# Conv products behind the query and key projections, four spread tiles in memory at once, scores ahead of the value projection

## The chip, the cores and the metric

One core of a Trainium2 chip runs the whole program. The time is device microseconds of one execution, and the median of three runs is compared. The core has five engines with an instruction queue each: TensorE (PE, matrix products), VectorE (DVE), ScalarE (ACT), GpSimd (POOL) and SyncE (SP, which here only issues loads). Each engine takes its instructions in order, and one that waits holds up all behind it. DMA transfers are issued from the queues of SP, ACT and POOL.

## The reference

One layer of an encoder with 256 tokens of width 1024, all in fp32. `mod` is six vectors of 1024 from the conditioning `c`.

```python
mod = silu(c) @ w_ada + b_ada                 # shift1, scale1, gate1, shift2, scale2, gate2
h = rms_norm(x, norm1_g) * (1 + scale1) + shift1
proj = h @ w_in                               # conv pair 2*512 | q 512 | k 512 | v 512
conv_out = conformer_conv(...)                # a*sigmoid(g), depthwise conv of width 31, layer norm, swish
attn_out = diff_attention(q, k, v, ...)       # 4 heads, normed q and k, two softmaxes each, p0 - lam * p1
x = x + gate1 * (concat([conv_out, attn_out]) @ w_out)
h2 = rms_norm(x, norm2_g) * (1 + scale2) + shift2
x = x + gate2 * routed_experts(h2, ...)       # top 4 of 32 experts, clamped SwiGLU, weights by softmax
```

## The kernel before

The order of instructions on each engine is the order in which the program is written (`manual_schedule` over all five engines). The front part, up to about 214.8 us, computes everything up to the routing; the rest runs the 32 experts one after the other.

**Weights.** All large weights come in chunks of 1 MB (`chunk`, L68; `wchunk`, L598), issued by SP in program order into rings of slots: `ringA` with 8 slots, `ringW` with 4, and from the close of `early` on `ringB` with 7. A load waits until the slot's former contents have been used, and the ones behind it wait too. An expert takes 12 chunks (8 of gate and up, 4 of down). The first experts' chunks go into slots that hold modulation weights (`ADA`), so `mod` frees them.

**Modulation.** `mod(s, q)` (L196) computes a quarter of vector s on DVE: two multiplies of 128x1024 with a running sum (L199) and a small add (L204). There are 24 of them, one for each ADA chunk, spread over the front part. The last six stand in the residual loop (`MODS`, L639).

**Conv.** The GLU writes `pad` (L320), one group of 128 channels j after another in the order `JS` = 2, 3, 1, 0. `spread(j)` (L264) copies a group into a tile `xs` by 16 small DMAs with four shifts, so that `conv(j)` (L272) can do the 31 taps as 32 short products on PE. Two `xs` buffers exist, so the third spread waits for the first conv. `spread(2)` is issued by ACT, the three others by POOL. `conv(j)` writes the one PSUM buffer `pc`, and ACT copies it to `acc`(L279); the next user of `pc` waits for that copy.

**Attention.** `proj(w, t)` (L334) projects q, k and v (w = 0, 1, 2) for two halves t of the tokens. `head_squares`, `head_norm` and `head_turn` normalise q and k and turn them; `scores`, `softmax`, `difference`, `turn_p` and `attend` do one head each. `out_proj(d, i, ...)` (L539) adds half i of the mix to output group d. In the last loop (L641) each d gets its second half, `residual(d)` on DVE adds it to x, `route(d)` on PE adds to the router's scores, and `add_squares` (L619) sums squares for the second norm.

**Biases of the experts.** `bgu` (32x2048, fp32) is split into three bfloat16 parts in `b3` (rows 0, 32 and 64): ACT copies the first part (L445), DVE subtracts it (L453), ACT copies the rest to `b3m` (the buffer named `osb`, L454), DVE subtracts again (L459), and ACT copies the remainder (L471).

Names in the trace: `pc` is the PSUM buffer of conv and of `turn_p`, `pq` that of the projections, of scores and of out_proj; `s` at L453 is `bgu`; `xT` also holds the residual.

Of the kernel before, what the change touches and what calls it, by code (L numbers as in the profile page):

```python
# [4 lines left out]
F32 = mybir.dt.float32  # L5
# [8 lines left out]
T = 256  # L14
# [17 lines left out]
def hybrid_layer(tc, xT_d, par_d, ada_d, win_d, wout_d, bgu_d, bdn_d, wgu_d, wdn_d, out_d):  # L32
# [44 lines left out]
    def load_ada(s, q):  # L77
        ADA[s, q] = chunk(ada_d[s, q])
# [14 lines left out]
    for q in range(4):  # L93
        load_ada(1, q)
        load_ada(0, q)
        WI[0, q] = chunk(win_d[q])
    for c in range(2):
        WI[1, c] = chunk(win_d[4 + c])
    load_ada(4, 0)
    load_ada(4, 1)  # L100
    nc.sync.dma_start(bgu, bgu_d)
    for c in range(2):
        WI[2, c] = chunk(win_d[6 + c])
    load_ada(4, 2)
    load_ada(4, 3)
    for c in range(2):
        WI[3, c] = chunk(win_d[8 + c])

    fold_w = [ringW.tile([128, 2048], F32, name="w") for i in range(2)]
    for q in range(4):  # L110
        load_ada(3, q)


    dgrid = mid.tile([128, 128], I32, name="dgrid")
# [107 lines left out]
    def scale1(q):  # L222
        ks = slice(2 * q, 2 * q + 2)
        V.scalar_tensor_tensor(a1[:, ks], modT[:, 1, ks], 1.0, pc("n1", 2 * q, 2 * q + 2), op0=OP.add, op1=OP.mult)

    r1 = rms_scale(ss1, 2, NT, "1")
    mod(1, 0)
    scale1(0)
    mod(0, 0)
    for i in range(12):  # L230
# [32 lines left out]

    def spread(j):  # L264

        XS[j] = early.tile([128, 4, T + 28], F32, name="xs", bufs=2)
        for i in range(4):
            for b in range(4):
                (nc.scalar if j == 2 else G).dma_start(XS[j][32 * i:32 * i + 32, b],
                                                       pad[32 * b:32 * b + 32, j, i:i + T + 28])  # L270

    def conv(j):  # L272
        pcn = ps_s.tile([128, T], F32, name="pc")
# [24 lines left out]
    for q in range(4):  # L298
        if q:
            mod(1, q)  # L300
            scale1(q)
            mod(0, q)
        norm_x(q)
        make_h(q)
        if q == 0:
            A.activation(dist, dist, AF.Abs)
        elif q == 1:
            for h in range(2):
                A.activation(alibi[:, h], dist, AF.Copy, scale=-SLOPES[h])
        elif q == 2:  # L310
            for h in range(2, 4):
                A.activation(alibi[:, h], dist, AF.Copy, scale=-SLOPES[h])
        else:
            table(AF.Sigmoid)
        for j in JS:
            conv_in(q, j)
            if q == 3:
                sg = early.tile([128, T], F32, name="qn", bufs=2)
                A.activation(sg, pcv[j][:, 1], AF.Sigmoid)
                V.tensor_mul(pad[:, j, 15:15 + T], pcv[j][:, 0], sg)  # L320
                if j in (2, 3):
                    spread(j)
                if j == 3:
                    make_folds(0)
    close(ps_c)
# [101 lines left out]
            TE.transpose(pt[:, t], osb[:, 2 * h + t], identf)  # L427
        A.activation(mixT[:, 4 + h], pt.rearrange("p a b -> p (a b)"), AF.Copy, scale=sg8)

    WO[0] = [chunk(wout_d[0, c], ringW) for c in range(2)]  # L430
    load_ada(2, 0)
    load_ada(2, 1)
    first, second = range(4), range(4, KD)
    proj(0, 0)
    mod(4, 0)
    head_squares(0, 0)
    conv(2)
    spread(1)
# [4 lines left out]
    V.tensor_scalar(sg8, pc("sg"), 1.0 - LAM0, None, op0=OP.mult)  # L443
    mod(4, 1)
    A.activation(b3[0:32], bgu, AF.Copy)  # L445
    proj(0, 1)
    conv(3)
    spread(0)
    mod(4, 2)
    head_squares(0, 1)  # L450
    head_norm(0)
    conv(1)
    V.tensor_sub(bgu, bgu, b3[0:32])  # L453
    A.activation(b3m, bgu, AF.Copy)  # L454
    mod(4, 3)
    proj(1, 0)
    for t in range(NT):
        head_turn(0, t)
    V.tensor_sub(bgu, bgu, b3m)  # L459
    A.activation(b3[32:64], b3m, AF.Copy)  # L460
    head_squares(1, 0)
    conv(0)
    mu = ps_s.tile([128, T], F32, name="po")
    for j in JS:
        TE.matmul(mu, mean512, acc[:, j], start=j == JS[0], stop=j == JS[-1])
    mod(3, 0)
    proj(1, 1, first)
# [3 lines left out]
    A.activation(b3[64:96], bgu, AF.Copy)  # L471
# [5 lines left out]
    mod(3, 1)  # L477
    proj(1, 1, second)
    WO[1] = [chunk(wout_d[1, c], ringW) for c in range(2)]
    load_ada(2, 2)  # L480
    load_ada(2, 3)
    for q in range(4):
        load_ada(5, q)
# [4 lines left out]
    head_squares(1, 1)  # L488
    head_norm(1)
    proj(2, 0, first)  # L490
    rbc = ps_s.tile([128, T], F32, name="po")
    for t in range(NT):
        TE.transpose(rbc[:, t * 128:t * 128 + 128], rv[:, t:t + 1].to_broadcast([128, 128]), identf)
    for j in range(4):
        V.tensor_mul(acc[:, j], acc[:, j], rbc)
        A.activation(sqc[:, j, :T], acc[:, j], AF.Sigmoid, scale=pc("lg", j), bias=pc("lb", j))
        V.tensor_scalar(acc[:, j], acc[:, j], pc("lg", j), pc("lb", j), op0=OP.mult, op1=OP.add)
    proj(2, 0, second)
    for t in range(NT):
        head_turn(1, t)  # L500
    for i in range(2):
        V.tensor_mul(lp[:, i], pc("lam", 128 * i, 128 * i + 64), pc("lam", 128 * i + 64, 128 * i + 128))
    V.tensor_reduce(lam, lp, axis=AX.X, op=OP.add)
    A.activation(lam, lam, AF.Exp)
    A.activation(vt[:, 0], PQ[2, 0], AF.Copy)
    for j in range(4):
        V.tensor_mul(mixT[:, j], acc[:, j], sqc[:, j, :T])
    PQ[2, 1] = ps_s.tile([128, 512], F32, name="pq", bufs=4)
    scores(0, "pq")
    scores(1, "pt")  # L510
    proj(2, 1)
    nlam = mid.tile([128, 1], F32, name="nlam")
    V.tensor_sub(nlam, lam[:, 1:2], lam[:, 0:1])
    V.tensor_scalar(nlam, nlam, -LAM0, None, op0=OP.add)
    softmax(0)
    softmax(1)
    mod(3, 2, (0,))
    difference(0)
    A.activation(vt[:, 1], PQ[2, 1], AF.Copy)
# [555 lines left out]
```

## Time and profile before

| | us |
|---|---|
| median of three runs | 1196.76 (1194.98, 1196.76, 1197.84) |
| profiled execution, its time | 1198.14 |
| its span | 1196.4 |
| PE busy | 1091.1 (91%) |
| DVE busy | 338.3 (28%) |
| ACT busy | 146.5 (12%) |
| POOL busy | 25.7 (2%) |
| first gate product of expert 0 | 214.81 |
| mean granted TensorE clock | 0.977 of full speed |

The busy shares are means over two very different parts. In the experts PE is nearly always busy; in the front part it is idle for some stretches and its granted clock falls to half in some of them, seen in products that take twice as long (L277: 64 products in 3.66 us or in 7.06). In a timeline row the first number is the start, the second the time from there to the end of the group, then engine, line, operation, output<-inputs, the size, the count, and in brackets the idle time before it with what ended it. A name with q behind the engine (SPq, ACTq) is its queue.

### The profile page before, as it was taken

How to read it: one execution, taken by the hardware profiler on the slowest of the kernel's cores; microseconds unless marked ns; L12 is line 12 of the kernel's file. 1: busy time of each engine (PE TensorE's matmuls, PEld its weight loads, DVE VectorE, ACT ScalarE, POOL GpSimd, SP SyncE). 2: the span in 40 equal slices, each digit the busy share in tenths (PEclk: the TensorE clock that was granted, in tenths of full speed). 3: DMA queues.
4: the chain of work that ended last, by engine and by line, in shares of the span. 5: the costliest groups of instructions: out<-in, count | busy, mean ns of one | idle time of the engine just before them, and what ended most of it. 6: DMA issues, size and time to landing. Idle time of an engine off the chain costs nothing. (4 is left out here: it accounts for less than half of the span.)

```text
span 1196.4 us, 13803 instructions
## 1 busy us (share of the span) xinstructions
PE 1091.1 (91%) x5387; PEld 498.3 (42%) x5387; DVE 338.3 (28%) x833; ACT 146.5 (12%) x301; POOL 25.7 (2%) x57
## 2 busy tenths in 40 slices
PE   7969878999999999998999999998988988898886
PEld 4625466534443344443444444443333333333332
DVE  7354667322222122221222222222111122222212
ACT  2013321110011000110000101000000000000000
POOL 0052000000000000000000000000000000000000
PEclk8978898999999999999999999999999999999999
DMA  9795528999999899997799999999999999999993
GB/s 376 274 344 200 207 102 318 421 419 420 419 419 422 337 412 419 421 420 298 296 414 420 418 419 420 420 419 421 419 420 420 419 421 419 419 420 419 419 401 133
DMA packets 65892, 449.36 MB, mean 376 GB/s; under 512 B 7984, under 2 KB 8496, under 8 KB 12240
## 3 DMA queue, kind: packets, MB, share of 16 engines
q1 hardware_dynamic: 63424, 445.27, 91.1%
q0 software_dynamic: 1584, 1.88, 0.5%
q8 instruction: 83, 1.36, 0.5%
q10 hardware_dynamic: 768, 0.58, 0.2%
q14 instruction: 33, 0.27, 0.1%
HBM read 444.33 MB, written 1.05 MB: 372 GB/s over the span
## 5 line engine op out<-in xcount | busy, mean ns | idle before, releaser
L772 PE MATMUL pu<-w,xg 128*64 128x512 f32 x1024 | 234.8, 597 | 19.8 <-DMA w<-in_wgu_dram 19.8
L772 PE MATMUL pg<-w,xg 128*64 128x512 f32 x1024 | 232.0, 597 | 13.0 <-DMA w<-in_wgu_dram 8.1
L813 PE MATMUL pd<-w,yT 128*64 128x512 f32 x992 | 218.1, 592 | 0.0
L772 PEld LDWEIGHTS pg<-w,xg 128*64 128x64 f32 x1024 | 79.2, 136 | 163.4 <-issue 139.8
L772 PEld LDWEIGHTS pu<-w,xg 128*64 128x64 f32 x1024 | 75.4, 136 | 153.2 <-issue 99.9
L813 PEld LDWEIGHTS pd<-w,yT 128*64 128x64 f32 x992 | 69.5, 137 | 127.9 <-issue 123.9
L965 DVE COPY o<-pd 64x512 f32<-64x512 f32 x31 | 21.2, 683 | 224.8 <-PE pd L813 224.8
L777 DVE TENSOR_SCALAR gp<-pg 128x512 f32<-128x512 f32 x34 | 23.5, 691 | 215.3 <-PE pg L772 215.3
L786 DVE TENSOR_SCALAR gp<-pu 128x512 f32<-128x512 f32 x32 | 22.1, 692 | 175.4 <-issue 163.6
L734 PEld LDWEIGHTS misc<-hot,xtok 128*128 128x128 f32 x496 | 57.8, 192 | 12.3 <-issue 12.2
L750 PE MATMUL y<-s,o 128*128 128x256 f32 x240 | 59.0, 389 | 4.2 <-PEq L947 0.6
L734 PE MATMUL misc<-hot,xtok 128*128 128x128 f32 x496 | 62.0, 278 | 0.0
L199 DVE SCALAR_TENSOR_TENSOR w<-w,crow 128x1024 f32<-128x1024 f32 x48 | 56.7, 1217 | 3.4 <-DMA w<-in_ada_dram 3.4
L750 PEld LDWEIGHTS y<-s,o 128*128 128x128 f32 x240 | 43.1, 189 | 16.3 <-issue 11.7
L967 ACT ACTIVATE o<-pd 64x512 f32<-64x512 f32 x31 | 18.4, 593 | 254.7 <-DVE o L965 254.7
L780 ACT ACTIVATE sg<-gp 128x512 f32<-128x512 f32 x32 | 20.1, 630 | 231.1 <-DVE gp L777 231.1
L338 PE MATMUL pq<-w,hT 128*128 128x512 f32 x96 | 42.9, 596 | 0.0
L277 PE MATMUL pc<-xs,w 128*32 128x256 f32 x256 | 23.7, 482 | 14.1 <-DVE pad L320 6.8
L542 PE MATMUL pq<-mixT,w 128*128 128x256 f32 x128 | 31.6, 398 | 5.1 <-DVE xT L613 5.1
L257 PE MATMUL cv<-hT,w 128*128 128x256 f32 x128 | 30.9, 408 | 5.6 <-DVE hT L246 5.6
L710 ACT ACTIVATE xg<-misc,modT,a 128x128 f32<-128x128 f32 x62 | 28.3, 457 | 45.9 <-DVE xg L712 45.9
L797 ACT ACTIVATE yT<-pu 128x256 f32<-128x256 f32 x32 | 12.3, 383 | 174.5 <-PEq L947 155.6
(291 smaller groups left out, 701.2 us busy)
## 6 DMA issues: line engine op xcount, KB each, us to landing
w<-in_wgu_dram SPq DMA_DIRECT2D x256, 1024.0 KB, 19.9
w<-in_wdn_dram SPq DMA_DIRECT2D x124, 1024.0 KB, 19.9
w<-in_ada_dram SPq DMA_DIRECT2D x24, 1024.0 KB, 10.8
w<-in_win_dram SPq DMA_DIRECT2D x10, 1024.0 KB, 12.3
w<-in_wout_dram SPq DMA_DIRECT2D x4, 1024.0 KB, 8.7
w<-in_wdn_dram SPq DMA_DIRECT2D x8, 512.0 KB, 14.5
xs<-pad POOLq DMA_DIRECT2D x48, 35.5 KB, 6.1
xT<-in_xT_dram SPq DMA_DIRECT2D x2, 512.0 KB, 5.8
```

The costliest lines, as they stand in the source:

```text
L199: V.scalar_tensor_tensor(w, w, 1.0, crow, op0=OP.mult, op1=OP.mult, accum_out=modT[:, s, 2 * q + i:2 * q + i + 1])
L257: TE.matmul(pcv[j][:, g], WI[0, q][:, o:o + 128], hT[:, k], start=k == 0 and g == 0, stop=k == KD - 1, skip_group_check=True)
L277: TE.matmul(pcn[32 * b:32 * b + 32], fold_w[j // 2][:, o:o + 32], XS[j][:, b, 4 * g:4 * g + T], start=g == 0, stop=g == 7)
L338: TE.matmul(PQ[w, t], hT[:, k, t * 128:t * 128 + 128], WI[1 + w, k // 4][:, (k % 4) * 512:(k % 4) * 512 + 512], start=k == 0, stop=k == KD ...
L542: TE.matmul(po4[d // 2][:, d % 2], WO[i][k // 2][:, o:o + 128], mixT[:, 4 * i + k], start=first and k == 0 and d % 2 == 0, stop=last and k ...
L710: A.activation(dst, src, AF.Identity, scale=a2[:, k:k + 1], bias=sh2[:, k:k + 1])
L734: TE.matmul(px[:, i], xtok[:, t, k * 128:k * 128 + 128], PP[p][:, t], start=t == 0, stop=t == NT - 1)
L750: TE.matmul(Y[d // 2][:, d % 2], O[p][:, d * 128:d * 128 + 128], S[p].rearrange("p a b -> p (a b)"), start=False, stop=False, skip_group_c ...
L772: TE.matmul(P[64 * n:64 * n + 64], xg[:, k], W[k // 2][:, o:o + 512], start=False, stop=k == KD - 1)
L777: V.tensor_scalar(gp, P, 7.0, None, op0=OP.min)
L786: V.tensor_scalar(y, P, -7.0, 7.0, op0=OP.max, op1=OP.min)
L813: TE.matmul(P[64 * n:64 * n + 64], yT[:, j, half * 64:half * 64 + 64], down_part(W, f, n), start=f == 0, stop=f == 7)
```

## The change

The code is written in another order and a few instructions change engine.

- `spread` writes groups 2 and 3 into `ringW` tiles and groups 1 and 0 into the two `xs` buffers, and is called for every group right behind its `pad`; all its DMAs are issued by POOL.
- All four `conv` calls stand behind the q and k projections: `conv(2)` and `conv(3)` behind `proj(1, 1)`, `conv(1)` behind the turn of k, `conv(0)` behind `scores(0)`. Scores 0 and 1 stand ahead of the value projections.
- The two subtractions of the bias split go from DVE to POOL; the affine step of the conv's norm goes from DVE to ACT.
- The modulations are placed earlier: the loop holds four of them (5, 0 to 3). The first is split, with one half ahead of the first norm chain. In the loop `add_squares` stands ahead of `residual`.
- The order of the loads follows; `WO[0]` is loaded into the slots that the two spread tiles held, `WO[1]` into those of the fold weights.
- `turn_p(2)` and `turn_p(3)` stand behind one out_proj pair each, `softmax(2)` behind the attends of the first two heads.

```diff
@@ loads @@
-    load_ada(4, 0)
-    load_ada(4, 1)
...
+    for w in (1, 2):
+        for c in range(2):
+            WI[w, c] = chunk(win_d[2 + 2 * w + c])
+        if w == 1:
+            nc.sync.dma_start(bgu, bgu_d)
+    for q in range(4):
+        load_ada(4, q)
+    load_ada(3, 0)
     for c in range(2):
         WI[3, c] = chunk(win_d[8 + c])
+    for q in range(1, 4):
+        load_ada(3, q)
+    load_ada(2, 0)
+    load_ada(2, 1)
@@ first norm @@
+    mod(1, 0, (0,))
     r1 = rms_scale(ss1, 2, NT, "1")
-    mod(1, 0)
+    mod(1, 0, (1,))
@@ def spread(j) @@
-        XS[j] = early.tile([128, 4, T + 28], F32, name="xs", bufs=2)
+        if j < 2:
+            XS[j] = early.tile([128, 4, T + 28], F32, name="xs", bufs=2)
+        else:
+            XS[j] = ringW.tile([128, 2048], F32, name="w")[:, :4 * (T + 28)].rearrange("p (b t) -> p b t", b=4)
...
-                (nc.scalar if j == 2 else G).dma_start(XS[j][32 * i:32 * i + 32, b],
-                                                       pad[32 * b:32 * b + 32, j, i:i + T + 28])
+                G.dma_start(XS[j][32 * i:32 * i + 32, b], pad[32 * b:32 * b + 32, j, i:i + T + 28])
...
-                if j in (2, 3):
-                    spread(j)
+                spread(j)
@@ projections @@
     A.activation(b3[0:32], bgu, AF.Copy)
+    G.tensor_tensor(bgu, bgu, b3[0:32], OP.subtract)
     proj(0, 1)
-    conv(3)
-    spread(0)
-    mod(4, 2)
     head_squares(0, 1)
     head_norm(0)
+    A.activation(b3m, bgu, AF.Copy)
+    G.tensor_tensor(bgu, bgu, b3m, OP.subtract)
+    proj(1, 0)
...
+    proj(1, 1)
+    A.activation(b3[32:64], b3m, AF.Copy)
+    A.activation(b3[64:96], bgu, AF.Copy)
+    head_squares(1, 1)
+    head_norm(1)
+    conv(2)
+    conv(3)
...
+    conv(1)
...
+    scores(0, "pq")
...
+    conv(0)
+    WO[0] = [chunk(wout_d[0, c], ringW) for c in range(2)]
+    load_ada(2, 2)
+    load_ada(2, 3)
+    WO[1] = [chunk(wout_d[1, c], ringW) for c in range(2)]
...
+    scores(1, "pt")
...
+    proj(2, 0, first)
...
+    proj(2, 1, first)
...
     for u in range(4):
         attend(u)
-    mod(3, 2, (1,))
+    softmax(2)
     softmax(3)
@@ residual loop @@
-    MODS = {0: (2, 2), 1: (2, 3), 3: (5, 0), 4: (5, 1), 6: (5, 2), 5: (5, 3)}
+    MODS = {0: (5, 0), 2: (5, 1), 4: (5, 2), 5: (5, 3)}
...
         out_proj(d, 1, range(4), last=True)
+        if before_d:
+            add_squares(before_d)
         residual(d)
```

POOL around the spreads, before (L269 is the spread, L610 a constant for the last norm):

```order
L118 IOTA sqq 128x512
L269 DMA xs<-pad 32x284 x48
L610 MEMSET ones_1128 128x1
L910 DMA o<-in_bdn_dram 32x1024
L927 UNCONDITIONAL_BRANCH
```

The same place after; s_85 is `bgu`, b_283 the tile `b3`, osb the tile `b3m`:

```order
L119 IOTA sqq 128x512
L274 DMA w<-pad 32x284 x32
L274 DMA xs<-pad 32x284 x32
L444 TENSOR_TENSOR s_85<-s_85,b_283 32x2048
L449 TENSOR_TENSOR s_85<-s_85,osb 32x2048
L616 MEMSET ones_1136 128x1
```

All 64 spread DMAs stand on POOL, and the two subtractions stand behind them.

ACT from the GLU's first sigmoid on, before (qn is the sigmoid, sqq a square of `head_squares`, acc the copy behind a conv, the rows into b_279 and osb the bias copies):

```order
L319 ACTIVATE qn<-cv_276 128x256
L269 DMA xs<-pad 32x284 x16
L319 ACTIVATE qn<-cv_277 128x256
L319 ACTIVATE qn<-cv_275 128x256
L319 ACTIVATE qn<-cv_274 128x256
L345 ACTIVATE sqq<-pq 128x512
L279 ACTIVATE acc<-pc,par 128x256
L445 ACTIVATE b_279<-s_85 32x2048
L279 ACTIVATE acc<-pc,par 128x256
L345 ACTIVATE sqq<-pq 128x512
L279 ACTIVATE acc<-pc,par 128x256
L454 ACTIVATE osb<-s_85 32x2048
```

ACT from the second square on, after:

```order
L348 ACTIVATE sqq<-pq 128x512
L448 ACTIVATE osb<-s_85 32x2048
L348 ACTIVATE sqq<-pq 128x512
L365 ACTIVATE qT<-pt,gq_290 128x4x128 x2
L461 ACTIVATE b_283<-osb 32x2048
L462 ACTIVATE b_283<-s_85 32x2048
L348 ACTIVATE sqq<-pq 128x512
L283 ACTIVATE acc<-pc,par 128x256 x2
L365 ACTIVATE kT<-pt,par 128x4x128 x2
```

The copies behind conv(2) and conv(3) (acc) stand behind the three bias copies that need the differences, where two of them stood ahead of the first such copy.

PE from the first projection on, before (pq is a projection, pc a conv, pt the turn of q, po a mean of the conv's norm):

```order
L338 MATMUL pq<-w,hT 128x512 x8
L277 MATMUL pc<-xs,w 32x256 x32
L338 MATMUL pq<-w,hT 128x512 x8
L277 MATMUL pc<-xs,w 32x256 x64
L338 MATMUL pq<-w,hT 128x512 x8
L360 MATMUL pt<-identf,qn 128x128 x8
L277 MATMUL pc<-xs,w 32x256 x32
L465 MATMUL po<-acc,mean_79 128x256 x4
```

The same place after (pc<-w is conv(2) and conv(3), whose spread tiles are slots named w; the second pt is the turn of k, the last pq are scores):

```order
L341 MATMUL pq<-w,hT 128x512 x24
L363 MATMUL pt<-identf,qn 128x128 x8
L341 MATMUL pq<-w,hT 128x512 x8
L281 MATMUL pc<-w 32x256 x64
L363 MATMUL pt<-identf,qn 128x128 x8
L281 MATMUL pc<-xs,w 32x256 x32
L375 MATMUL pq<-kT,qT 128x256 x4
```

All four projections of q and k stand ahead of the first conv.

DVE in the residual loop, before (L613 is the residual, L199 and L204 a modulation, L620 the sum of squares):

```order
L613 SCALAR_TENSOR_TENSOR xT<-pq,modT,xT 128x256
L199 SCALAR_TENSOR_TENSOR w,modT<-w,crow 128x1024 x2
L204 TENSOR_TENSOR modT<-modT,par 128x2
L613 SCALAR_TENSOR_TENSOR xT<-pq,modT,xT 128x256
L199 SCALAR_TENSOR_TENSOR w,modT<-w,crow 128x1024 x2
L204 TENSOR_TENSOR modT<-modT,par 128x2
L613 SCALAR_TENSOR_TENSOR xT<-pq,modT,xT 128x256
L620 TENSOR_TENSOR s2all<-s2all,s_1144 128x256
L613 SCALAR_TENSOR_TENSOR xT<-pq,modT,xT 128x256
```

The same place after:

```order
L619 SCALAR_TENSOR_TENSOR xT<-pq,modT,xT 128x256
L200 SCALAR_TENSOR_TENSOR w,modT<-w,crow 128x1024 x2
L205 TENSOR_TENSOR modT<-modT,par 128x2
L619 SCALAR_TENSOR_TENSOR xT<-pq,modT,xT 128x256
L626 TENSOR_TENSOR s2all<-s2all,s_1152 128x256
L619 SCALAR_TENSOR_TENSOR xT<-pq,modT,xT 128x256
L200 SCALAR_TENSOR_TENSOR w,modT<-w,crow 128x1024 x2
L205 TENSOR_TENSOR modT<-modT,par 128x2
```

Two of the six modulations left the loop, and the sum of squares stands ahead of the next residual.

## Rows read from the trace of the kernel before

**Rows 1.** waits of PE, 215 to 820 (line waited for: us, times, longest).
```profile
PE misc L762 <- ACT xg L710: 5.5, 2, 2.7
```

**Rows 2.** timeline of PE (start, us, instructions, idle before).
```profile
214.81 5.32 PE L772 MATMUL pg<-w,xg 128*64 128x512 f32 x24
...
348.34 7.09 PE L772 MATMUL pg<-w,xg 128*64 128x512 f32 x32 [0.17 <-PEq L968]
```

**Rows 3.** waits of the load queue SPq, 300 to 410.
```profile
SPq L600 <- PE pd L813: 17.0, 2, 16.7
```

**Rows 4.** busy time by stretch: PE, PEld, DVE, ACT, POOL, PEclk, DMA share, GB/s.
```profile
400.00:420.00 20.00, 18.90 (x92) 7.59 (x90) 3.21 (x9) 1.22 (x2) 0.00 (x0) 1.00 0.73 293
600.00:1160.00 560.00, 518.39 (x2494) 208.37 (x2490) 118.47 (x272) 51.75 (x105) 0.00 (x0) 1.00 1.01 419
```

**Rows 5.** timeline of SPq, issues of loads.
```profile
59.47 3.83 SPq L70 DMA_DIRECT2D w<-in_ada_dram  x2
...
73.82 21.36 SPq L70 DMA_DIRECT2D w<-in_ada_dram  x4
...
320.63 17.70 SPq L600 DMA_DIRECT2D w<-in_wgu_dram  x8
```

**Rows 6.** page, section 6: issues, KB each, us from issue to landing.
```profile
w<-in_wgu_dram SPq DMA_DIRECT2D x256, 1024.0 KB, 19.9
```

**Rows 7.** waits of PE, 45 to 214.
```profile
PE pc L277 <- DVE pad L320: 6.8, 1, 6.8
PE pc L277 <- DMA xs<-pad: 6.6, 2, 6.2
PE pq L542 <- DVE xT L613: 5.1, 2, 4.2
```

**Rows 8.** timeline of ACT, 45 to 100.
```profile
45.99 14.11 ACTq L269 DMA_DIRECT2D xs<-pad  x16
...
98.68 1.89 ACT L454 ACTIVATE osb<-s 32x2048 bf16<-32x2048 f32 x1
```

**Rows 9.** timeline of POOL, 0 to 100.
```profile
1.33 0.59 POOL L118 IOTA sqq<- 128x512 f32 x1
61.29 4.07 POOL L269 DMA_DIRECT2D xs<-pad  x8 [59.38 <-DVE pad L320]
...
72.19 1.08 POOL L269 DMA_DIRECT2D xs<-pad  x2 [0.39 <-DMA xs<-pad]
...
91.35 5.91 POOL L269 DMA_DIRECT2D xs<-pad  x12 [0.29 <-DMA xs<-pad]
```

**Rows 10.** timeline of DVE.
```profile
10.93 0.16 DVE L125 TENSOR_SCALAR rm<-ss 128x2 f32<-128x2 f32 x1 [1.83 <-PE ss L218]
...
90.26 2.27 DVE L453 TENSOR_TENSOR s<-s,b 32x2048 f32<-32x2048 f32 x1
```

**Rows 11.** page, section 5: groups (busy us, mean ns, idle before).
```profile
L199 DVE SCALAR_TENSOR_TENSOR w<-w,crow 128x1024 f32<-128x1024 f32 x48 | 56.7, 1217 | 3.4 <-DMA w<-in_ada_dram 3.4
...
L338 PE MATMUL pq<-w,hT 128*128 128x512 f32 x96 | 42.9, 596 | 0.0
```

**Rows 12.** timeline of PE, 80 to 185.
```profile
81.32 3.66 PE L277 MATMUL pc<-xs,w 128*32 128x256 f32 x64
91.21 7.06 PE L277 MATMUL pc<-xs,w 128*32 128x256 f32 x64 [6.22 <-DMA xs<-pad]
...
145.20 1.13 PE L372 MATMUL pq<-kT,qT 64*128 64x256 f32 x8
...
151.03 7.07 PE L542 MATMUL pq<-mixT,w 128*128 128x256 f32 x32
159.01 0.41 PE L405 MATMUL pc<-identf,s 128*128 128x128 f32 x2 [0.91 <-DVE s L397]
...
173.27 1.97 PE L542 MATMUL pq<-mixT,w 128*128 128x256 f32 x8
179.42 3.50 PE L542 MATMUL pq<-mixT,w 128*128 128x256 f32 x8 [4.18 <-DVE xT L613]
```

More of the change, by code (lines that the diff above doesn't have):

```diff
@@ L96, in hybrid_layer @@
         WI[0, q] = chunk(win_d[q])
-    for c in range(2):
-        WI[1, c] = chunk(win_d[4 + c])
-    load_ada(4, 0)
-    load_ada(4, 1)
[L101 to L105, printed above, removed]
+    for w in (1, 2):
[6 more added lines that the diff above has]
+    load_ada(3, 0)
     for c in range(2):
         WI[3, c] = chunk(win_d[8 + c])
+    for q in range(1, 4):
+        load_ada(3, q)
+    load_ada(2, 0)
+    load_ada(2, 1)
     fold_w = [ringW.tile([128, 2048], F32, name="w") for i in range(2)]
-    for q in range(4):
-        load_ada(3, q)
     dgrid = mid.tile([128, 128], I32, name="dgrid")
@@ L428, in head_mix @@
         A.activation(mixT[:, 4 + h], pt.rearrange("p a b -> p (a b)"), AF.Copy, scale=sg8)
-    WO[0] = [chunk(wout_d[0, c], ringW) for c in range(2)]
-    load_ada(2, 0)
-    load_ada(2, 1)
     first, second = range(4), range(4, KD)
@@ L436, in hybrid_layer @@
     head_squares(0, 0)
-    conv(2)
-    spread(1)
     V.tensor_scalar(identb, dgrid, 0.0, None, op0=OP.is_equal)
@@ L445, in hybrid_layer @@
     A.activation(b3[0:32], bgu, AF.Copy)
+    G.tensor_tensor(bgu, bgu, b3[0:32], OP.subtract)
     proj(0, 1)
-    conv(3)
-    spread(0)
-    mod(4, 2)
     head_squares(0, 1)
     head_norm(0)
-    conv(1)
-    V.tensor_sub(bgu, bgu, b3[0:32])
     A.activation(b3m, bgu, AF.Copy)
-    mod(4, 3)
+    G.tensor_tensor(bgu, bgu, b3m, OP.subtract)
     proj(1, 0)
+    mod(4, 2, (0,))
+    head_squares(1, 0)
     for t in range(NT):
         head_turn(0, t)
-    V.tensor_sub(bgu, bgu, b3m)
-    A.activation(b3[32:64], b3m, AF.Copy)
-    head_squares(1, 0)
-    conv(0)
+    mod(4, 2, (1,))
+    mod(4, 3)
+    for i in range(2):
+        V.tensor_mul(lp[:, i], pc("lam", 128 * i, 128 * i + 64), pc("lam", 128 * i + 64, 128 * i + 128))
+    V.tensor_reduce(lam, lp, axis=AX.X, op=OP.add)
+    proj(1, 1)
+    A.activation(b3[32:64], b3m, AF.Copy)
+    A.activation(b3[64:96], bgu, AF.Copy)
[3 more added lines that the diff above has]
+    conv(3)
+    mod(3, 0)
+    mod(3, 1)
+    mod(3, 2, (0,))
+    for t in range(NT):
+        head_turn(1, t)
+    conv(1)
+    PQ[2, 0] = ps_s.tile([128, 512], F32, name="pq", bufs=4)
+    PQ[2, 1] = ps_s.tile([128, 512], F32, name="pq", bufs=4)
+    scores(0, "pq")
+    A.activation(lam, lam, AF.Exp)
+    nlam = mid.tile([128, 1], F32, name="nlam")
+    V.tensor_sub(nlam, lam[:, 1:2], lam[:, 0:1])
+    V.tensor_scalar(nlam, nlam, -LAM0, None, op0=OP.add)
+    softmax(0)
+    mod(3, 2, (1,))
+    conv(0)
+    WO[0] = [chunk(wout_d[0, c], ringW) for c in range(2)]
+    load_ada(2, 2)
+    load_ada(2, 3)
+    WO[1] = [chunk(wout_d[1, c], ringW) for c in range(2)]
+    for q in range(4):
+        load_ada(5, q)
     mu = ps_s.tile([128, T], F32, name="po")
@@ L465, in hybrid_layer @@
         TE.matmul(mu, mean512, acc[:, j], start=j == JS[0], stop=j == JS[-1])
-    mod(3, 0)
-    proj(1, 1, first)
+    scores(1, "pt")
     V.tensor_sub(acc, acc, mu[:, None, :].to_broadcast([128, 4, T]))
@@ L470, in hybrid_layer @@
     A.activation(sqc[:, :, :T], acc, AF.Square)
-    A.activation(b3[64:96], bgu, AF.Copy)
+    proj(2, 0, first)
     vsr = ps_s.tile([128, T], F32, name="po")
@@ L476, in hybrid_layer @@
     A.activation(vrow, vsr, AF.Copy)
[L477 to L483, printed above, removed]
+    softmax(1)
+    difference(0)
+    mod(3, 3)
+    proj(2, 0, second)
+    A.activation(vt[:, 0], PQ[2, 0], AF.Copy)
     vs = ps_s.tile([128, 2], F32, name="po")
@@ L487, in hybrid_layer @@
     rv = rms_scale(vs, 1, NT, "c")
-    head_squares(1, 1)
-    head_norm(1)
-    proj(2, 0, first)
+    difference(1)
+    table(AF.Sigmoid)
+    proj(2, 1, first)
     rbc = ps_s.tile([128, T], F32, name="po")
@@ L496, in hybrid_layer @@
         A.activation(sqc[:, j, :T], acc[:, j], AF.Sigmoid, scale=pc("lg", j), bias=pc("lb", j))
[L497 to L505, printed above, removed]
+    turn_p(0)
+    for j in range(4):
+        A.activation(acc[:, j], acc[:, j], AF.Identity, scale=pc("lg", j), bias=pc("lb", j))
+    mod(2, 0)
+    proj(2, 1, second)
+    A.activation(vt[:, 1], PQ[2, 1], AF.Copy)
     for j in range(4):
         V.tensor_mul(mixT[:, j], acc[:, j], sqc[:, j, :T])
[L508 to L519, printed above, removed]
+    table(AF.Exp)
+    turn_p(1)
     scores(2, "pq")
-    turn_p(0)
-    difference(1)
     scores(3, "pt")
-    turn_p(1)
-    softmax(2)
     for u in range(4):
         attend(u)
-    mod(3, 2, (1,))
+    softmax(2)
     softmax(3)
@@ L549, in hybrid_layer @@
         out_proj(d, 0, range(4), True)
+    turn_p(2)
+    difference(3)
     next_po()
@@ L552, in hybrid_layer @@
         out_proj(d, 0, range(4), True)
-    difference(3)
-    turn_p(2)
+    mod(2, 1)
+    turn_p(3)
     next_po()
-    for d in (4, 5):
-        out_proj(d, 0, range(4), True)
-    turn_p(3)
+    out_proj(4, 0, range(4), True)
     for u in range(4, 8):
         attend(u)
+    out_proj(5, 0, range(4), True)
     head_out(1)
@@ L566, in hybrid_layer @@
         head_mix(h)
-    mod(3, 3)
+    mod(2, 2)
     V.scalar_tensor_tensor(a2, modT[:, 4], 1.0, pc("n2"), op0=OP.add, op1=OP.mult)
@@ L578, in hybrid_layer @@
                   start=k == 0, stop=k == KD - 1)
-    mod(2, 0)
-    mod(2, 1)
+    mod(2, 3)
     V.tensor_add(rbias, sb, pc("br"))
@@ L647, in hybrid_layer @@
             route(before_d)
-            if before_d:
-                add_squares(before_d)
         before_d = d
```

## Prediction

> **What bounds the kernel now.** I read the waits of TensorE (PE) first, in the expert part. From 215 to 820 us its longest wait is 5.5 us in two pieces, on ScalarE (ACT), and no weight load stands in that list [rows 1]: PE sets the pace there. Next, who waits for PE: in 300 to 410 the load queue (SP) stood 17.0 us on PE's down products [rows 3], and the DMA engines were 0.73 busy in 400 to 420 [rows 4], where an expert runs a second block of tokens: the weight rings were full and the loads could not run ahead. After 600 the DMA is at 1.01 [rows 4]; from there loads set the pace. So the loads of the last part start when PE frees slots at the extra blocks, and that is a fixed distance behind the first gate product of expert 0, at 214.81 [rows 2]. If that product comes X us earlier, the end comes X us earlier, as long as weights still arrive ahead of PE. The tightest place I found is expert 5: its load group was issued from 320.63 on [rows 5], a load lands 19.9 us after its issue [rows 6], so 340.5, and is used at 348.34 [rows 2]: 7.8 us to spare. If the loads move earlier as much as the products, the 7.8 stays; if they don't move, X counts only to 7.8.
>
> The change touches only the front part. There PE's largest waits are 6.8 us on the padded GLU outputs (the spreads' source), 6.6 on spread DMAs and 5.1 on the residual in the last loop [rows 7]. All three are touched.
>
> **Start.** VectorE (DVE) idles 1.83 us ahead of the first norm chain [rows 10]. Half of a modulation, 1.2 us [rows 11], now fills it. One of its two multiplies leaves the path, less the handover: 0.8 earlier (0 to 1.2).
>
> **Spreads.** ACT spent 14.11 us issuing 16 spread DMAs [rows 8] while the sigmoids of the next groups waited behind it, which is PE's 6.8. Now GpSimd (POOL) issues all 64, each group right behind its pad, and no tile is waited for. POOL's pace is seen twice: 16 from 61.29 to 73.27, 0.75 each, while weight loads are in flight, and 12 in 5.91, 0.49 each, in a stretch with little loading [rows 9]. Loads came at about 3.6 us each beside spreads (two in 3.83, and 14.35 us from 59.47 to 73.82 for four of them [rows 5]); some ten stand in the queue from 46 on until the ring is full, so I take loaded pace until about 76. POOL starts at 45.99 − 0.8 = 45.2: 30.8/0.75 = 41 spreads by 76, 23 more at 0.49 = 11.3, end at **87.3** (76.6 if all go at 0.49; 93.2 if all at 0.75).
>
> **The added wait.** The two subtractions on the experts' biases, 2.27 us each on DVE [rows 10], are now on POOL, behind all 64 spreads. ACT's copy of the first difference waits for it, and ACT runs in order: behind it stand the square of k's first half, two turns of q, two bias copies (one waits for the second subtraction), another square and the conv sums' copies. PE's conv(3) needs the sum buffer that the copy of conv(2) frees. So PE, done with the four q and k projections and conv(2) by about 82, waits. No row shows a POOL subtraction. From below: DVE's 2.27. From above: three times four IOTA of 512, 0.59 each [rows 9], = 7.1. I take two reads at that rate, 2 × 4 × 0.59 = 4.7, since IOTA is the only POOL arithmetic here. Two such plus ACT's copies: 4.7 + 1.89 [rows 8] + 4.7 + 1.9 + 0.6 + 0.5 (a bias copy as the first, then a square and a sum copy, both short) = 14.3; conv(3) starts at **101.6** (87.5 with spreads to 76.6, a first subtraction of 2.27 and, in place of a second one so short, ACT's own work up to the last bias copy, about 3.8: a square, two turns, a copy; 112.3 with 93.2 and 7.1 each). Cover behind the wait: DVE's reduction of the held square and two modulations stand there too, and SP stops when the ring is full.
>
> The Trainium skill, GPSIMD Engine Reference, section 3.1, gives 4497 ns for an fp32 tensor_tensor add of 2048 on GpSimd and 2293 ns on VectorE; the 2.27 us of VectorE in this trace agrees, and no row shows the other. By that page, an estimate, conv(3) would come 0.4 us earlier. Its section 4.1 names VectorE for such elementwise work, which speaks against this part of the change.
>
> **From conv(3) to out_proj(0,1).** PE was idle, so conv(3) runs at half clock: 7.06, as before after an idle of 6.22; two more convs 3.66 each [rows 12]; the four half projections of v are 32 products at 42.9/96 us = 14.3 [rows 11]; scores 2 and 3, two turns and four attends 5.8 (145.20 to 151.03), out_proj(0,1) half of 7.07 = 3.5 [rows 12]; scores 0 and 1, a turn of k, and the small products of the conv's norm, 7.2 together by the length of the like blocks (an estimate). Sum 7.06 + 7.3 + 14.3 + 5.8 + 3.5 + 7.2 = 45.2, so **146.8**. The conv's norm, which used to hold PE nowhere long, lies beside the v projections; DVE's modulations have room there.
>
> **To the residual loop.** Before, the third head's turn came at 159.01, 8.0 after out_proj began at 151.03: 7.07 of products and 0.91 idle, in which ACT and DVE finished that head's softmax [rows 12]. Its softmax now stands behind the attends and only 3.5 of product lies in that gap: 8.0 − 3.5 = 4.5 idle, and a half-clock stretch after it, 1.5 (8 products took 3.50 after an idle of 4.18, but 1.97 without [rows 12]). Then the work that took 159.01 to 173.27 = 14.3 [rows 12] plus the out_proj(2,3) that moved behind, 3.5: 17.8. Loop starts at 146.8 + 6.0 + 17.8 = **170.6** (before 173.27).
>
> **The loop.** Before, from 173.27 to the first gate product at 214.81: 41.5. It loses the idle of 4.18 (DVE was two modulations behind) and its half clock 1.5, and two of six modulations, 2 × 2.6 (two multiplies at 1.22 [rows 11] and an add), as DVE is the loop's bound there; the sum of squares goes ahead of the residual and saves nothing. About ten handovers between PE and DVE, now both waiting in turn, cost 0.1 each: +1.0. 41.5 − 4.2 − 1.5 − 5.2 + 1.0 = 31.6; first gate product at **202.2**, X = 12.6. The last modulation that frees a slot stays inside this loop, so the loads move about as much.
>
> **How the numbers follow.** The profiled execution took 1198.14 us, its span 1196.4, so 1.74 lie outside. 1198.14 − 12.6 = 1185.5 in its own terms; the median of the runs is 1.38 lower, 1196.76 − 12.6 = **1184.2**. With the known scatter of the terms (0.8 for the start, 2 for conv(3), 3 for the wait ahead of the loop, 3 for the loop) the forecast's own range is 1178 to 1191. Chance 0.58.
>
> Rivals:
> - POOL is quick. Speaks for it: 0.49 per spread and 0.59 for 512 elements [rows 9]. conv(3) at 87.5, 14.1 earlier; DVE then has the modulations of the stretch left as it is and takes some of it back, about 1: X = 25.7, **1171**. Chance 0.14.
> - POOL is slow, yet not decisive: conv(3) at 112.3, 10.7 later, X = 1.9: **1194.9**. Chance 0.10.
> - Slower: the POOL chain takes more than it gives. The gain is gone when conv(3) starts after 101.6 + 12.6 = 114.2. With all spreads at 0.75 (end 93.2) and 4.9 for ACT's copies that is a subtraction of (114.2 − 93.2 − 4.9)/2 = 8.05 us; at 10 us each conv(3) starts at 93.2 + 20 + 4.9 = 118.1, **1200.7**. For it: the spreads of before never ran long at 0.49 before 91 [rows 9]. Against it: 8.05 is 3.5 times DVE's time. Chance 0.11.
> - The loads don't move: SP is stopped behind the out-projection weights, which now wait for conv(3)'s tiles, and the expert weights come as late as now. X counts 7.8: **1189**. For it: their queue is in order. Against it: after conv(3) at about 109 some 14 loads of 3.6 us stand before the first expert weights, 50 us, to about 159, while the modulations that free the slots of the last of them run in the loop anyway. Chance 0.03.
> - It does not do what it says: PE's idle time only moves from the spreads to ACT's copy, and the loop is bound by PE after all, so that 9.4 and 1.5 do not come: X = 12.6 − 9.4 − 1.5 = 1.7, or 0 with conv(3) two later: **1196.8**. Chance 0.04.
>
> 0.2% is 2.4 us, about what a measurement of this kernel can tell from no change. Faster: 0.58 + 0.14 + 0.03 and most of the 0.10, 0.83; within 0.2%: 0.05; slower: 0.12. The range 1170 to 1197 holds all but the slower case and a bit at the quick end.
>
> **What would show it.** POOL: last spread near 87, two subtractions of 4 to 5 us. ACT: idle from about 62 to 92 in the bias copy. PE: idle from about 82, conv(3) near 101.6 at half clock, out_proj(0,1) ending near 147, an idle of 4.5 us ahead of the third turn, the loop near 170.6, first gate product near 202, and a wait for residuals in the loop under 2 us. In the expert part: the same pace, shifted by X, expert 5 with 7 us to spare. Wrong if subtractions take over 8 us, if the conv's norm or DVE's queue holds the v stretch, if a lower clock stays after the long idle, or if expert weights show up among PE's waits before 820.

## The result, and the profile after

The changed kernel takes 1183.85 us in the median of four runs (1179.83 to 1184.32), the kernel before 1196.51 beside it (1194.98 to 1197.84). The ratio is 0.9887, with a 95% interval from 0.9863 to 0.9912. The prediction was 1184.2. The profiled execution took 1183.91 us with a span of 1182.1.

The waits of PE in the front part, 45 to 205 us (line waited for: us in total, times, longest), are no longer those of [rows 7]:

```profile
PE pc L281 <- ACT acc L283: 23.1, 1, 23.1
PE pc L408 <- DVE s L400: 4.3, 2, 4.0
...
PE pq L548 <- DVE xT L619: 1.0, 2, 0.8
PE po L636 <- DVE s2all L626: 0.5, 1, 0.5
```

The 6.8 us on pads and the 6.6 on spreads are gone, the 5.1 on the residual have become 1.0, and one wait of 23.1 us has come in their place: conv(3) waits for ACT's copy of conv(2). Two more waits of the kernel before, which [rows 7] leave out, are gone or short as well, the one on k's turn and the one on the sum of squares in the last loop:

```profile
PE pq L372 <- ACT kT L362: 4.8, 1, 4.8
PE po L630 <- DVE s2all L620: 2.5, 1, 2.5
```

With so long a new wait the kernel is still faster. The timeline of POOL shows where that wait begins; it answers to [rows 9]:

```profile
45.42 4.08 POOL L274 DMA_DIRECT2D w<-pad  x8 [43.50 <-DVE pad L324]
52.35 0.50 POOL L274 DMA_DIRECT2D w<-pad  x1 [2.85 <-DMA w<-pad]
...
81.93 9.38 POOL L274 DMA_DIRECT2D xs<-pad  x19 [0.15 <-issue]
91.32 4.07 POOL L444 TENSOR_TENSOR s<-s,b 32x2048 f32<-32x2048 f32 x1
97.40 4.05 POOL L449 TENSOR_TENSOR s<-s,osb 32x2048 f32<-32x2048 f32 x1 [2.02 <-ACT osb L448]
```

POOL needs from 45.42 to 91.3 for 64 spreads, then 4.07 us for the first subtraction. ACT's timeline, which answers to [rows 8], shows the queue behind it:

```profile
63.19 0.60 ACT L348 ACTIVATE sqq<-pq 128x512 f32<-128x512 f32 x1 [4.48 <-PE pq L341]
95.42 1.91 ACT L448 ACTIVATE osb<-s 32x2048 bf16<-32x2048 f32 x1 [31.63 <-POOL s L444]
...
101.48 1.91 ACT L462 ACTIVATE b<-s 32x2048 bf16<-32x2048 f32 x1 [0.61 <-POOL s L449]
...
103.91 0.47 ACT L283 ACTIVATE acc<-pc,par 128x256 f32<-128x256 f32 x1
```

ACT stood 31.63 us in front of a bias copy. The copy of conv(2), written behind it, could only run at 103.91, though conv(2) had been ready since 81.3. PE's timeline follows, with the places that answer to [rows 12] and [rows 2]:

```profile
77.69 3.66 PE L281 MATMUL pc<-w 128*32 128x256 f32 x64
104.43 6.31 PE L281 MATMUL pc<-w 128*32 128x256 f32 x64 [23.08 <-ACT acc L283]
...
144.94 3.62 PE L548 MATMUL pq<-mixT,w 128*128 128x256 f32 x16
152.53 0.41 PE L408 MATMUL pc<-identf,s 128*128 128x128 f32 x2 [3.97 <-DVE s L400]
...
171.07 1.97 PE L548 MATMUL pq<-mixT,w 128*128 128x256 f32 x8
173.80 1.99 PE L548 MATMUL pq<-mixT,w 128*128 128x256 f32 x8 [0.76 <-DVE xT L619]
...
202.61 5.32 PE L778 MATMUL pg<-w,xg 128*64 128x512 f32 x24
```

After conv(3) no wait of PE is longer than the 3.97 us at 152.53: the first gate product stands at 202.61 instead of 214.81, X = 12.2. The residual wait of 4.18 us in the loop is 0.76 here.

### The profile page after: what moved, and what is told of

Same layout as the page of the kernel before. It is cut to its first block, busy times and chain, and to the rows that moved or that the text cites. A ratio compares the mean times of both kernels' runs of the same rounds, so it can differ in the third digit from the quotient of the medians.

```text
span 1182.1 us, 13810 instructions
## 1 busy us (share of the span) xinstructions
PE 1077.9 (91%) x5387; PEld 496.0 (42%) x5387; DVE 335.8 (28%) x827; ACT 151.0 (13%) x309; POOL 41.7 (4%) x75
## 5 line engine op out<-in xcount | busy, mean ns | idle before, releaser
L740 PEld LDWEIGHTS misc<-hot,xtok 128*128 128x128 f32 x496 | 57.8, 192 | 12.7 <-issue 12.2
L200 DVE SCALAR_TENSOR_TENSOR w<-w,crow 128x1024 f32<-128x1024 f32 x48 | 59.8, 1279 | 10.3 <-DMA w<-in_ada_dram 10.3
L281 PE MATMUL pc<-w 128*32 128x256 f32 x128 | 10.0, 471 | 23.1 <-ACT acc L283 23.1
```

The costliest lines, as they stand in the source:

```text
L740: TE.matmul(px[:, i], xtok[:, t, k * 128:k * 128 + 128], PP[p][:, t], start=t == 0, stop=t == NT - 1)
```

## The experiments

The ratio of each is to the kernel before, measured beside it. A time is compared with the changed kernel through that ratio, or directly where both were measured beside the same runs of the kernel before; the first gate product is that of the profiled execution.

### The changed kernel once more

> The changed kernel once more, as the mark for the three others. Both theories: 0.989 of the kernel before, first gate product near 202.6.

It measured 0.9907 (0.9888 to 0.9927), 1184.26 us, first gate product 201.55. So the mark is 0.989 to 0.991, and the first gate product varies by about 1 us between executions.

### The subtractions back on DVE

```diff
-    G.tensor_tensor(bgu, bgu, b3[0:32], OP.subtract)
+    V.tensor_sub(bgu, bgu, b3[0:32])
...
-    G.tensor_tensor(bgu, bgu, b3m, OP.subtract)
+    V.tensor_sub(bgu, bgu, b3m)
```

> The changed kernel with the two bias subtractions back on DVE, at the same places of the program. Theory (the 23.1 us in which PE waits for ACT's copy of conv(2) comes from POOL's late subtractions through ACT's queue, and counts in full at the end): ACT's bias copy no longer stands still from 63 to 95, conv(3) starts right behind conv(2) near 81.5, conv(0) waits for the last spreads until about 95 instead of 117, so the first gate product comes about 21 us earlier, near 182, and the time is about 1163. Rival (the stall is mostly covered: DVE's modulations or the loads would hold PE instead): less than 4 us, 1180 or more.

It measured 0.9820 (0.9799 to 0.9840), some 9 us below the changed kernel, and the first gate product came at 192.39, 10.2 earlier. The theory is half right. PE's wait of 23.1 us for ACT is gone, but another has come, as its waits and its timeline show:

```profile
PE pc L281 <- DMA xs<-pad: 8.1, 3, 6.4
```

```profile
102.56 6.75 PE L281 MATMUL pc<-xs,w 128*32 128x256 f32 x64 [6.36 <-DMA xs<-pad]
```

conv(0) started at 102.56, not 95, and took 6.75 us instead of 3.66, near half clock. The spreads ended later here, at 99.3 instead of 91.3. The busy time by stretch (columns as in [rows 4]) points to the loads, first of the changed kernel, then of this one:

```profile
70.00:80.00 10.00, 10.00 (x69) 5.04 (x70) 0.00 (x0) 0.00 (x0) 5.85 (x12) 1.00 0.86 268
82.00:91.00 9.00, 0.00 (x0) 0.00 (x0) 0.00 (x0) 0.00 (x0) 8.91 (x19) 0.70 0.28 73
```

```profile
82.00:99.00 17.00, 12.10 (x146) 7.57 (x146) 9.53 (x19) 5.27 (x13) 9.12 (x19) 1.00 1.03 347
```

With the DMA engines at 0.28, POOL issued 19 spreads in 9 us; with them at 0.86 or 1.03, 12 in 10 and 19 in 17. DVE was idle in both stretches of the changed kernel, so DVE isn't what slows them. An issue itself takes POOL 0.50 in either case. The first eight followed each other in 4.08 us, and the ninth, at 52.35, waited for an earlier spread to land. From issue to landing a spread into `xs` took 1.8 us in the changed kernel and 6.7 in this run (pages, section 6):

```profile
xs<-pad POOLq DMA_DIRECT2D x32, 35.5 KB, 1.8
```

```profile
xs<-pad POOLq DMA_DIRECT2D x32, 35.5 KB, 6.7
```

If eight can be under way at once, 6.7/8 = 0.84 us a spread follows, about the pace seen; this is an estimate from these rows, and no run varies the eight. In the changed kernel the stall of ACT had stopped DVE at the square it waits for, and with it the modulation that frees the next slot; the waits of the load queue between 60 and 110 show it:

```profile
SPq L70 <- DVE w L200: 40.4, 2, 38.8
```

So the last spreads were quick: the wait gave back part of its own price.

### The bias copies later on ACT

```diff
-    A.activation(b3m, bgu, AF.Copy)
-    G.tensor_tensor(bgu, bgu, b3m, OP.subtract)
     proj(1, 0)
...
-    A.activation(b3[32:64], b3m, AF.Copy)
-    A.activation(b3[64:96], bgu, AF.Copy)
...
     conv(1)
+    A.activation(b3m, bgu, AF.Copy)
+    G.tensor_tensor(bgu, bgu, b3m, OP.subtract)
+    A.activation(b3[32:64], b3m, AF.Copy)
+    A.activation(b3[64:96], bgu, AF.Copy)
```

> The changed kernel with the subtractions still on POOL, but ACT's three later bias copies (and so the second subtraction) written behind conv(1), so that no square and no conv copy stands behind them. Theory (ACT's order, not POOL's time, makes the wait): conv(3) starts near 81.5, and the next thing late is the first softmax, whose exponentials on ACT stand behind the last bias copy, near 103.5 instead of 118.5: 15 us earlier, about 1169. Rival (what counts is that POOL ends its work late): no more than 4 us gained, 1180 or more.

It measured 0.9888 (0.9869 to 0.9906): no gain that the comparison can tell; the first gate product stood at 198.95, 3.7 earlier. conv(3) did start at 81.77, as the theory said, so ACT's order makes that wait. But the 15 us did not come. The timelines of ACT and PE:

```profile
102.34 1.91 ACT L469 ACTIVATE osb<-s 32x2048 bf16<-32x2048 f32 x1 [8.18 <-POOL s L444]
...
108.43 1.91 ACT L472 ACTIVATE b<-s 32x2048 bf16<-32x2048 f32 x1 [2.24 <-POOL s L470]
```

```profile
101.59 6.95 PE L281 MATMUL pc<-xs,w 128*32 128x256 f32 x64 [6.34 <-DMA xs<-pad]
...
115.28 1.22 PE L491 MATMUL po<-acc,mean 128*128 128x256 f32 x2 [5.25 <-ACT acc L283]
```

Loads went on, the spreads ended at 98, so POOL's subtractions came 7 us later than in the changed kernel; the first softmax, which writes over the buffer of `bgu` (`s`), stood behind the copies, and the copy of conv(0) behind the softmax. The wait only moved on along ACT's queue. Both the order on ACT and POOL's end count.

### More work on POOL

```diff
+    for i in range(2):
+        G.tensor_tensor(acc[0:32].rearrange("p a b -> p (a b)"), bgu[:, :1024], b3[0:32, :1024], OP.subtract)
     G.tensor_tensor(bgu, bgu, b3[0:32], OP.subtract)
```

> The changed kernel with two more subtractions of half the size on POOL ahead of the first bias subtraction, writing to a tile that is overwritten later: 2 x 2.05 = 4.1 us more on POOL. Theory (POOL's end, ACT's queue, the copy of conv(2) and the first gate product are one chain): conv(3) starts at 108.5, first gate product 4.1 later, 206, time 4.1 above the changed kernel, 1188. Rival (DVE's queue or the loads hold the part behind conv(3), so that PE's wait has slack): less than 1.5 above.

It measured 0.9953 (0.9937 to 0.9969), 6 to 7 us above the changed kernel. The timelines of POOL and PE:

```profile
92.56 4.32 POOL L445 TENSOR_TENSOR acc<-s,b 32x1024 f32<-32x1024 f32 x2
96.96 4.04 POOL L446 TENSOR_TENSOR s<-s,b 32x2048 f32<-32x2048 f32 x1
```

```profile
110.05 5.21 PE L281 MATMUL pc<-w 128*32 128x256 f32 x64 [28.88 <-ACT acc L283]
```

In this execution the spreads ended 1.2 later than in the first profile; with 4.3 for the two additions that is 5.5 at POOL, 5.6 at conv(3) (110.05 against 104.43), and 4.5 at the first gate product (207.07). The 1.1 between the last two is the clock: conv(3) took 5.21 here and 6.31 in the first profile. So from POOL to the first gate product there is one chain, without slack that these rows show. The profiled execution was 6.4 above the first one, 4.5 of it from there and 1.7 from expert 5, of which more below.

### spread(2) on ACT again

```diff
-                G.dma_start(XS[j][32 * i:32 * i + 32, b], pad[32 * b:32 * b + 32, j, i:i + T + 28])
+                (nc.scalar if j == 2 else G).dma_start(XS[j][32 * i:32 * i + 32, b],
+                                                       pad[32 * b:32 * b + 32, j, i:i + T + 28])
```

> The changed kernel with spread(2) issued by ACT again, as before the change. Theory (what counts of the spreads is only when POOL reaches the subtractions): POOL starts near 60.5 with 48 spreads, 21 of them at 0.75 until 76 and 27 at 0.49, ends at 89.5 instead of 91.3; conv(3) no later than 104.4, time within 2 us of the changed kernel. Rival (ACT's 14 us cost what they cost before, since the sigmoids and the first square stand behind them): 5 to 7 us more, 1189.

1186.54 us, 2.3 above the changed kernel measured beside it (0.9937, 0.9916 to 0.9958, against 0.9907, 0.9888 to 0.9927; the intervals overlap). POOL began at 58.18 and reached the first subtraction 1.8 us later than in the changed kernel, not earlier, as the theory had it:

```profile
93.14 4.07 POOL L445 TENSOR_TENSOR s<-s,b 32x2048 f32<-32x2048 f32 x1
```

conv(3) started at 106.25, 1.8 later, and the first gate product came at 204.41, also 1.8 later. So the theory missed POOL's end by 3.6 us (93.1 instead of 89.5), but held in what counts: the later end of POOL comes out at the first gate product. ACT's issuing (12.46 us here) makes PE wait 4.2 for q's turn, as against 6.8 for the pads before [rows 7, 8], and these 4.2 lie ahead of the long wait for ACT's copy, which is 19.5 instead of 23.1.

### The late modulations where they stood

First, all but (3,3):

```diff
-    MODS = {0: (5, 0), 2: (5, 1), 4: (5, 2), 5: (5, 3)}
+    MODS = {0: (2, 2), 1: (2, 3), 3: (5, 0), 4: (5, 1), 6: (5, 2), 5: (5, 3)}
```

with (2,0) and (2,1) behind the router's bias products and the four earlier calls taken out.

> The changed kernel with the modulations of gate1 where they stood before: (2,0) and (2,1) behind the router's bias products, (2,2) and (2,3) and the four of gate2 in the residual loop. Theory (the loop is bound by DVE, and two modulations fewer in it and two fewer just ahead of it are worth 4.2 + 1.5 + 5.2 - 1.0 = 9.9 us): first gate product near 212.5, time about 1193.8. Rival (the loop is bound by PE or by the chain between the engines; the gain of the change comes from the conv and attention part): within 2 us of the changed kernel, 1184 to 1186.

It measured 0.9966 (0.9949 to 0.9983), some 8 us above the changed kernel; first gate product 208.50, 5.9 later. That lies between the two. In this profile PE's longest wait for a residual in the loop was 1.89, not 4.18 as in [rows 12]. So the undoing was not whole; with (3,3) also behind the first two head mixes, as before the change:

> The changed kernel with every late modulation where it stood before: (3,3) behind the first two head mixes as well, (2,0) and (2,1) behind the router's bias products, (2,2), (2,3) and gate2's four in the loop. Theory (the earlier undoing of modulations gave 5.9 us instead of 9.9 at the first gate product because (3,3) had stayed early, so that DVE was one modulation less behind when the loop began): the wait of about 4 us for the first residuals is back with its half-clock products, first gate product near 202.2 + 9.9 = 212, time about 10 above the changed kernel, 1194. Rival (the loop was worth no more than that run showed): first gate product near 208.5, 6 above, 1190.

It measured 0.9982 (0.9968 to 0.9996), 10 us above the changed kernel, and 1193.99 us where 1194 was expected. PE's timeline:

```profile
171.93 1.97 PE L546 MATMUL pq<-mixT,w 128*128 128x256 f32 x8
177.14 2.40 PE L546 MATMUL pq<-mixT,w 128*128 128x256 f32 x8 [3.23 <-DVE xT L617]
...
211.78 0.60 PE L776 MATMUL pg<-w,xg 128*64 128x512 f32 x2
```

The wait for the first residuals is back (3.23), and from the loop's start to the first gate product 39.9 us pass instead of 31.5. With the modulations late, nearly all of the change's gain is gone: it is the gain of this placement, and the rest of the change, taken together with its long wait, comes out nearly even. The placement doesn't need that wait: with the subtractions on DVE the loop takes the same 31.5 (160.84 to 192.39).

### difference(2) ahead of head_out(0)

```diff
-    head_out(0)
     difference(2)
+    head_out(0)
```

> The changed kernel with difference(2) written ahead of head_out(0) on DVE. Theory (the idle of 3.97 us ahead of the third head's turn is DVE's norm chain of head_out(0), which stands ahead of the difference, and the half-clock products behind it are its second price, 1.7): both go, about 5.5 us, time near 1178.4. Rival (the exponentials on ACT end last there, or the head's mix waits for the later norm chain): under 1.5 us, 1182.5 to 1184.

0.9869 (0.9851 to 0.9886), about 3 us below the changed kernel, while the first gate product came at 196.98, 5.6 earlier, as the theory said: the third head's turn follows out_proj without a wait.

```profile
144.88 3.62 PE L548 MATMUL pq<-mixT,w 128*128 128x256 f32 x16
148.34 0.60 PE L408 MATMUL pc<-identf,s 128*128 128x128 f32 x4
```

What is missing at the end in its profile is the clock (below): its first expert took 30.23 us instead of 28.57 and expert 10 took 62.73 instead of 61.14.

### Both edits, and half a spread on ACT

First the two edits of the subtractions on DVE and of the difference together:

> The subtractions on DVE and difference(2) ahead of head_out(0), together. Theory (the front part's chain is one chain, and what the first gate product gains the end gains): first gate product 192.4 - 5.6 = 186.8, time 15.8 below the changed kernel, about 1166. Rival (from here the expert weights come no earlier, or the clock takes the second part back): the second edit adds nothing, 8 to 10 below the changed kernel, about 1173.

1168.48 us, 0.9785 (0.9764 to 0.9806), 15.8 below the changed kernel measured beside it; first gate product 186.60. What the first gate product gains, the end gains. Then, in addition:

```diff
-                G.dma_start(XS[j][32 * i:32 * i + 32, b], pad[32 * b:32 * b + 32, j, i:i + T + 28])
+                (nc.scalar if j == 0 and i >= 2 else G).dma_start(XS[j][32 * i:32 * i + 32, b],
+                                                                  pad[32 * b:32 * b + 32, j, i:i + T + 28])
```

> The kernel with both edits, and in addition 8 of the 16 DMAs of spread(0) issued by ACT, which idles there. Theory (POOL issues one spread after the other at 0.75 us while loads are in flight, so its count sets the end): POOL ends 6 us earlier, conv(0) waits no more than 1 us and is not slowed by the clock, first gate product near 180, time about 6 below the kernel with both edits, 1160. Rival (the pace is that of the shared DMA engines, whoever issues): conv(0) starts where it did, near 102, and the time is within 1.5 us of the kernel with both edits.

1161.97 us, 0.9728 (0.9709 to 0.9747): the fastest version here. The timelines of ACT and PE:

```profile
49.53 13.58 ACTq L274 DMA_DIRECT2D xs<-pad  x8
```

```profile
97.41 3.66 PE L282 MATMUL pc<-xs,w 128*32 128x256 f32 x64
...
177.57 5.32 PE L779 MATMUL pg<-w,xg 128*64 128x512 f32 x24
```

conv(0) runs at 97.41 without a wait and at full clock. The first gate product is 9.0 earlier than with both edits alone, the time 6.5 lower. POOL's last spread was issued at 89.8 instead of 99.3. Part of that is the smaller count: eight spreads at 0.83 are 6.6 us, an estimate. Part is that the loads stood for a while; the load queue's wait, then the busy time in a stretch around its end:

```profile
SPq L70 <- DMA w<-in_ada_dram: 23.5, 1, 23.5
```

```profile
64.20:69.10 4.90, 4.90 (x12) 1.90 (x10) 4.87 (x12) 1.81 (x2) 4.86 (x10) 1.00 0.59 175
```

POOL issued ten spreads in 4.9 us there, with the DMA engines at 0.59, though PE and DVE were both busy throughout; in the version with both edits it issued six in this stretch, with the DMA engines at 1.01. So it is the loads that slow the spreads, and not the compute engines. From 71 to 90 the DMA engines were at 1.03 as before. How much of the gain is the second queue and how much the standing loads, no run separates. Eight issues took ACT 13.58 us, which held its first square up, and PE waits 4.2 for q's turn instead; that was cheaper.

## Why the prediction was right, point by point

**The bound** held. The first gate product moved by 12.2 and the end with it; expert 5's loads were issued from 310.58 and used at 336.07, which with 19.9 for the landing [rows 6] leaves 5.6 us to spare (7.8 before):

```profile
310.58 17.89 SPq L606 DMA_DIRECT2D w<-in_wgu_dram  x8
```

```profile
336.07 7.09 PE L778 MATMUL pg<-w,xg 128*64 128x512 f32 x32 [0.16 <-PEq L974]
```

In the twelve profiles the span ends 979.2 to 984.4 us behind the first gate product (981.6 before, 979.5 after), while that product moves from 177.57 to 214.81. One of the prediction's own signs of being wrong did show: expert weights stand among PE's waits before 820.

```profile
PE pu L778 <- DMA w<-in_wgu_dram: 1.8, 4, 0.5
...
PE pg L778 <- DMA w<-in_wgu_dram: 0.5, 1, 0.5
```

It is 2.3 us in five waits, all from 790 on; before, such waits begin at 823.89. There loads set the pace anyway, as the prediction said of the part after 600, and with the product 12.2 earlier the part begins earlier.

**Start** was forecast 0.8 earlier. The GLU's first product stood at 18.94 instead of 19.35, 0.4 earlier, but at 19.79 in the repeated run: the half modulation that was to fill the gap waited for its own weights (0.73 and 2.15 us). Over all eleven profiles with the change it stood between 18.61 and 19.79, so this term is not shown beyond the scatter.

**Spreads.** POOL started at 45.42 (45.2 was forecast), but ended at 91.3 instead of 87.3: beside loads a spread took 0.83 (12 in 10 us) and not 0.75, and loads were in flight until about 80, not 76. 91.3 lies inside the bounds of 76.6 and 93.2.

**The added wait** was seen in kind and place. A subtraction took 4.07 where 4.7 was taken, and the whole from the first subtraction to conv(3) 13.1 instead of 14.3. With the later spreads conv(3) started at 104.43, 2.8 behind the forecast.

**From conv(3) to out_proj(0,1)**: 104.43 to 148.56 = 44.1, forecast 45.2; no wait of PE in it.

**To the loop**: 148.56 to 171.07 = 22.5, forecast 23.8. The idle ahead of the third turn was 3.97 (4.5 forecast). Its cause is DVE's norm chain of head_out(0) ahead of the difference, which the prediction had left to softmax in general; putting the difference first removed it.

**The loop**: 171.07 to 202.61 = 31.5, forecast 31.6, and the last experiment on the modulations puts 8.4 of its gain of 10.0 back; what gives the other 1.6 no run shows. The parts of this term are less sure than its sum: a wait of 0.76 for a residual stayed where the forecast took all 4.18 away, and the wait on the sum of squares, for which it counted nothing, fell from 2.5 to 0.5 (1.8 with all modulations late). The 1.0 for handovers stands in no row. So four errors, +2.8 at conv(3), −1.1, −1.3 and −0.1, cancel to +0.4 at the first gate product. That the forecast lies 0.35 us from the median owes something to luck: the term of the spreads alone was off by 4.

**Not foreseen** was that X is not all of the difference between the two profiles: the spans differ by 14.3, not 12.2. 1.7 of the rest stands in expert 5, in the same products of before and after:

```profile
379.47 8.76 PE L772 MATMUL misc<-w,more 128*64 128x512 f32 x32
```

```profile
367.20 7.06 PE L778 MATMUL misc<-w,more 128*64 128x512 f32 x32
```

Before, the granted clock was 0.89 around these products (377 to 393); after, 1.00. Both came after the same idle of 2.74 us. It is a matter of the execution, not of the change: across the profiles expert 5 takes 59.9 or 61.6 us, and 61.6 in the repeated run of the changed kernel too. The medians of the runs, 1196.51 and 1183.85, differ by 12.7.

**The rivals.** The quick POOL fell with the end of the spreads at 91.3. Both slow ones, 7.1 and 10 us a subtraction, fell with 4.07. The loads moved (the first expert weights were issued at 140.54, before at 175.60), so that rival fell too. That the idle only moves and the loop gives nothing is the nearest to a part of the truth: without the early modulations the change gives next to nothing, as the run with all of them late shows (0.9982), but the loop does. That is so only with the subtractions on POOL: with them on DVE the conv part gains about 9 us more.

## What to carry to other kernels

Work that is moved to a free engine takes its place behind all that engine has queued, and what reads it on an in-order engine holds everything written behind the reader: look at who stands behind the waiting copy, not at how long the moved instruction takes. A long new wait may stand beside a real gain, so undo the parts one by one; here the half of the change that looks like its core came out nearly even, and the modulations moved out of the last loop and from just ahead of it carried the gain. And a stage that waits may be paying part of its price back by leaving the DMA to others; taking the wait away brings less than its length.

## What the hardware showed beside that

A DVE multiply of 1.22 us took 4.10 while POOL subtracted:

```profile
98.44 4.10 DVE L200 SCALAR_TENSOR_TENSOR w<-w,crow 128x1024 f32<-128x1024 f32 x1
```

POOL's second subtraction ran from 97.40 to 101.45, and the multiply ended 1.1 us after it; the same 4.10 appears in the repeated run and, 5.6 later, in the run with more work on POOL. The Trainium skill, SBUF — State Buffer, section "Who interferes with whom", says that a VectorE instruction with two inputs in SBUF contends with a GpSimd instruction that reads SBUF, and calls the port pair that they share an exclusive lock; the row agrees. It cost nothing here, since k's norm was done at 110.1 and its turn on PE began at 110.67.

The granted clock also fell inside experts, with no wait of PE longer than 0.2 us. The first expert, busy time of PE by stretch with the granted clock behind it, in the run with the subtractions on DVE and in the changed kernel:

```profile
192.39:224.29 31.90, 31.43 (x140) 0.89 1.02 421
```

```profile
202.61:231.18 28.57, 28.10 (x141) 1.00 1.01 420
```

At 0.89 it took 3.3 us more for the same products. Such stretches of 1.7 or 3.3 us come and go between executions, and the lowest and the highest run of one kernel lie 1 to 8 us apart; a profile that has one in it can hide an edit of that size.
